# Two-layer hybrid decoder on one core: side work of the attention heads moved to other ticks, q and k of layer 1 transposed as soon as they are scaled

## The chip, the cores and the metric

One core of a Trainium2 chip runs the whole program as one launch. The metric is the device time of that launch in microseconds. Engines: TensorE (PE; its weight loads are shown as PEld), VectorE (DVE), ScalarE (ACT), GpSimd (POOL) and SyncE (SP), which issues most DMAs. Each engine works off its own list of instructions in order.

## The reference

256 positions, model width 2048, two layers, a final RMSNorm, all in fp32. Cut to what matters:

```python
def layer_even(x, norm_g, w_in, w_out):            # layer 0
    h = rmsnorm(x, norm_g)
    qa, ka, va, iq, ik, iw, qb, kb, vb, gate = split_cols(h @ w_in, SPLIT0)
    o_a = dsa_attention(...)      # 10 heads; an indexer picks 64 keys per query
    o_b = dilated_attention(...)  # 6 heads; softmax over strided windows
    return x + (concat(o_a, o_b) * silu(gate)) @ w_out

def layer_odd(x, norm_g, w_in, b_f, w_out):        # layer 1
    h = rmsnorm(x, norm_g)
    qc, kc, vc, qd, kd, vd, fl, gate = split_cols(h @ w_in, SPLIT1)
    o_c = stick_breaking_attention(qc, kc, vc)     # 8 heads
    log_f = log_sigmoid(fl + b_f)
    o_d = forgetting_attention(qd, kd, vd, log_f)  # 8 heads
    return x + (concat(o_c, o_d) * silu(gate)) @ w_out

# stick breaking, per query and head, over the keys before it:
#   z = q.k / sqrt(128); tail = sum of log_sigmoid(-z) over later keys
#   w = exp(log_sigmoid(z) + tail);  o = w @ v
# forgetting: softmax(q.k / sqrt(128) + c[query] - c[key]) @ v, c = cumsum(log_f)
```

## The kernel before

**Jobs.** The projections are cut into jobs, each for the columns of one head (q, k, v, gate: 512 columns) or of some other group: in layer 0 `B0 K I0 I1 B1 B2 B3 A0 A2 A4 A6 A8 B4 B5` (an A job holds q and gate of two heads; K and I belong to the indexer), then `P0` to `P3`, the four column blocks of the output projection; in layer 1 `C0 F1 G1 C2 ... C7 D0 ... D7`, then `Q0` to `Q3`. F1 and G1 are the two halves of head C1; F1 also carries the forget gates. `project` runs one job: 16 steps over the contraction (kt), each with six matmuls of up to 512 columns. fp32 accuracy comes from splitting weights and activations each into a high part and a remainder: `hi x xh`, `hi x xl`, `lo x xh` (lines 324, 325, 327) for two blocks of 128 positions.

**Weights.** SP loads them in pieces of four kt (`raw`, three buffers). `split` turns a half piece (two kt) into `whi` on ACT (line 283) and `wlo` on DVE (line 284), four buffers each, three halves ahead of PE. A piece's buffer is loaded again by a DMA that is put in line four ticks after its second half was split (`later`).

**Ticks.** After each kt of a 512-column job PE's instruction stream has a tick. Between ticks a head's side work is put in line, by generators: `start` runs one up to its first `yield n`, and `advance` resumes it n ticks later. So all engines' lists hold the side work at places counted in ticks; nothing at run time moves an instruction past another one on its engine. After odd kts (two kt are one half) the next `split` follows: an even tick stands in front of a split, an odd one in the middle of a half.

**A head** (`head_b`, `heads_a`, `head_c`, `head_cf`, `head_d`) begins when its job's projection is done (its tick 0) by emptying the two PSUM accumulators: q and k scaled into `qk` (`scaled_qk`, layer 1) or rotated (`rotate`, layer 0), v and the gate (`vg1`: exp on ACT, reciprocal on DVE, `u`). Then q and k are transposed by way of DRAM: DVE transposes 32x32 blocks into `far` (`far`, line 418), SP stores `far` to DRAM (`fard`, line 420) and loads it back in the turned order into `qk` (line 422); `qk_parts` splits it into high part and remainder (`qkh`, `qkf` on ACT, `qkl` on DVE). The gate `u` goes the same way (`gate_turned`). The last head of each layer (B5, D7) has its q, k and gate transposed on PE instead (`turn`).

**Softmax heads** (A, B, D): scores on PE into PSUM tile `s`; `soft` adds the bias, takes the row extreme (`sn`, `nm` on DVE) and the exponential (ACT); `share` scales with the reciprocal row sum (`sc`, DVE); `turn` transposes `sn` on PE into `tp`; `cut` makes `ph` (ACT) and `pl` (DVE), and ACT copies `p1`; `weigh_out` multiplies with v into PSUM tile `o`, DVE multiplies by the gate (`uT`), and `cut` writes `yh` (ACT) and `yl` (DVE), the output projection's input. **Stick heads** (C, `stick_head`): scores into `s`; `z` on DVE, three functions on ACT, `sp` on DVE, `sph` (ACT) and `spl` (DVE); a second group on PE for the running sums; `z` again, exponential, `ph` (ACT), `pl` (DVE); `weigh_out`. The tiles `s`, `o`, `qkf`, `qkh`, `qkl`, `ph`, `pl`, `p1` have one buffer each; `tp` has two. ACT and DVE take turns where both read one accumulator or one turned tile.

`forget` makes the forget gates' running sum on PE; `forget_bias` prepares a D head's bias.

Of the kernel before, what the change touches and what calls it, by code (L numbers as in the profile page):

```python
# [14 lines left out]
P = 128  # L15
# [16 lines left out]
YPOS = {}  # L32
# [141 lines left out]
def trunk(ctx, tc, x, xT, g1, w0, wo0, w1, wo1, bf, gf, consts, rope, out):  # L174
# [232 lines left out]

    def far(srcs, dst, first, done, stored):

        yield first  # L410
        t = hp.tile([P, 512], F32, name="far", tag="rt2")
        ns = [x.shape[1] // P for x in srcs]
        n = sum(ns)
        d = dr.tile([P, P * n], F32, name="fard", tag=f"fard{n}", bufs=4)
        o = t[:, 0:P * n].rearrange("p (j b c) -> p b j c", j=4, b=n)
        for i, x in enumerate(srcs):
            b = sum(ns[:i])
            nc.vector.transpose(o[:, b:b + ns[i]], x.rearrange("p (b j l) -> p b j l", j=4, l=32))  # L418
        yield done
        nc.sync.dma_start(d, t[:, 0:P * n])  # L420
        yield stored
        nc.sync.dma_start(dst.rearrange("p (i f) -> p i f", i=4),
                          d.rearrange("r (j f) -> (r j) f", j=4).rearrange("(i q) f -> q i f", i=4))

    def qk_turned(qk, last, more=0):

        if last:
            yield last
            r = qk_parts(quarters(turn([qk[:, i * P:(i + 1) * P] for i in range(4)])))
            yield 6 - last  # L430
        else:
            yield from far([qk], qk, 1, 3, 4)
            yield 7
            r = qk_parts(arrived(qk, 4))
            yield 3 + more
        return qk_of(r)
# [87 lines left out]

    def softmax_head(qk, nb, v, u, rs, kt, last):
        uT = None if last else gate_turned(u)
        qk = yield from qk_turned(qk, last)
        pr, l = soft(qk, nb() if callable(nb) else nb)
        yield 2
        share(pr, factor(l, rs))  # L530
        yield 2 if last else 4
        pt = turn([pr[:, 0:P], pr[:, P:SEQ], pr[:, SEQ:384]])
        ph = hp.tile([P, SEQ], F32R, name="ph", tag="ph", bufs=1)
        pl = hp.tile([P, SEQ], F32R, name="pl", tag="pl", bufs=1)
        p1 = hp.tile([P, P], F32, name="p1", tag="p1", bufs=1)
        cut((ph, pl), pt[:, 0:SEQ])
        nc.scalar.activation(p1, pt[:, SEQ:384], AF.Copy)
        if last:
            uT = gate_turned_here(u)
        yield 2 if last else 3  # L540
        weigh_out(ph, pl, p1, v, uT, kt, False)
# [57 lines left out]
    def head_b(ps, h):  # L599
# [15 lines left out]
        last = 4 * (h == HB - 1)  # L615
        yield from softmax_head(qk, bmask, v, u, hr0, YPOS[f"B{h}"], last)

# [89 lines left out]
    def heads_a(ps, h):  # L707
# [11 lines left out]
        uT = gate_turned(u.rearrange("p a b c -> p (a b c)"), 4)  # L719
        yield from far([qk], qk, 1, 3, 4)  # L720
        yield 7
        q = arrived(qk, 4)
# [5 lines left out]
        nc.vector.tensor_tensor(quarters(lo), q[:, 2:4], quarters(hi).bitcast(F32), op=OP.subtract)  # L728
        yield 3
        js = [slice(j * P, (j + 1) * P) for j in range(2)]  # L730
# [108 lines left out]
    def forget(ps):  # L839
# [11 lines left out]
        nc.vector.scalar_tensor_tensor(flat(logf), flat(z), 0.0, flat(e), op0=OP.min, op1=OP.subtract)  # L851
        yield 5
        pc = pa.tile([P, 512], F32, name="s", tag="s", bufs=1)
# [23 lines left out]
    def stick_head(qk, v, uT, kt):  # L877
# [23 lines left out]
        pl = hp.tile([P, SEQ], F32R, name="pl", tag="pl", bufs=1)  # L901
        nc.scalar.activation(ph, z[:, P:384], AF.Copy)
        yield 1
        nc.vector.tensor_tensor(pl, z[:, P:384], ph.bitcast(F32), op=OP.subtract)
        yield 3
        weigh_out(ph, pl, z[:, 0:P], v, uT, kt, True)

    def stick(qk, v, u, kt):
        uT = gate_turned(u)
        t = yield from qk_turned(qk, False, 2)  # L910
        yield from stick_head(t, v, uT, kt)

    def head_c(ps, h):
        qk = scaled_qk(ps, 0, (2, 1), (3, 0))
        v, u = yield from vg1(ps, 256, h == 0)
        yield from stick(qk, v, u, h)

    def head_cf(ps, qk):
        v, u = yield from vg1(ps, 0)
        yield from stick(qk, v, u, 1)  # L920

    def head_d(ps, h):
        qk = scaled_qk(ps, 1, (0, 3), (1, 2))
        v, u = yield from vg1(ps, 256)
        last = 3 * (h == HDD - 1)
        yield from softmax_head(qk, lambda: biases[h], v, u, None, HC + h, last)

# [51 lines left out]
    for ji, (_, _, name, _) in enumerate(jobs):  # L979
# [26 lines left out]
        elif k == "I":  # L1006
            start(both(index(ps, h), best()) if h else index(ps, h))
        elif k == "A":
            start(heads_a(ps, h))
        elif k == "P":  # L1010
            start(feed1(ps, h))
        elif k == "F":
            held = scaled_qk(ps, 0, (2, 1), (3, 0))
            start(forget(ps))
        elif k == "G":
            start(head_cf(ps, held))
        elif k == "C":
            start(head_c(ps, h))
        elif k == "D":
            start(head_d(ps, h))  # L1020
        elif k == "Q" and h < 3:
            residual(ps, 2, h)
            start(gain(h))
# [35 lines left out]
```

## Time and profile before

| | |
|---|---|
| median of 3 runs | 917.76 us (917.73 to 918.2) |
| profiled execution | 918.31 us, of which the span shown is 916.5 us |
| PE busy | 897.2 us, 98% |
| DVE, ACT, POOL busy | 644.5, 476.4, 48.7 us |
| granted TensorE clock, mean | 0.994 |
| DMA | 194.20 MB, mean 212 GB/s |

Times in the profile count from the span's start. Matmuls are pipelined and their ends are modelled, so the distance between starts tells more of them than their durations. A row's idle time in brackets is that of the engine just before it, with what ended it. A granted clock of 1.00 is 2.4 GHz, half of it 1.2 GHz.

### The profile page before, as it was taken

Reading aid. Unit: us, or ns where it says so; the run is one execution under the profiler, and the core shown is the slowest. Engines: PE = TensorE matmul, PEld = TensorE weight load, DVE = VectorE, ACT = ScalarE, POOL = GpSimd, SP = SyncE. Lnnn points to the kernel's source line nnn. Section 1 sums busy time; section 2 is a strip of 40 time slices with the busy share of each in tenths; the row PEclk is TensorE's granted clock in tenths of the full one; section 3 lists DMA queues with packets and bytes.
Section 4 is the critical chain, followed back from the end, with each engine's and each line's share of the span. In section 5 each row is a group of like instructions: output and inputs, shape, how many; then the busy total and the mean of one; then the engine's idle time right before and its main releaser. Section 6 shows DMA issues by size and latency. Waiting matters only on the chain.

```text
span 916.5 us, 11926 instructions
## 1 busy us (share of the span) xinstructions
PE 897.2 (98%) x4295; PEld 749.7 (82%) x4295; DVE 644.5 (70%) x1136; ACT 476.4 (52%) x834; POOL 48.7 (5%) x71
## 2 busy tenths in 40 slices
PE   9999999999999998999999999999999999998996
PEld 6988888888888887888898788888778888887886
DVE  7667888777777775666667777767777777775563
ACT  7655544555555554554455555554555555554450
POOL 0021100000000000000000000000000000001110
PEclk9999999999999999999999999999999999999998
DMA  9974455675656653666586666665666666664542
GB/s 356 350 263 148 174 219 186 210 248 207 218 197 216 212 201 138 230 230 230 164 287 230 217 193 202 215 203 190 209 208 229 240 220 219 217 201 138 184 184 92
DMA packets 67355, 194.20 MB, mean 212 GB/s; under 512 B 15952, under 2 KB 38624, under 8 KB 49376
## 3 DMA queue, kind: packets, MB, share of 16 engines
q1 hardware_dynamic: 65856, 190.14, 59.2%
q0 software_dynamic: 864, 2.12, 0.9%
q10 hardware_dynamic: 576, 1.19, 0.4%
q8 instruction: 33, 0.54, 0.2%
q14 instruction: 26, 0.21, 0.1%
HBM read 178.61 MB, written 14.82 MB: 211 GB/s over the span
## 4 chain that ended last, share of the span: by engine, by line
PE 77%; DVE 10%; ACT 5%; issue 4%; DMA 3%; POOL 0%; SPq 0%; DVEq 0%; POOLq 0%; ACTq 0%
PE pj L324 24%; PE pj L325 24%; PE pj L327 24%; DVE wlo L284 4%; ACT whi L283 3%; DVE e L829 2%; PE tp L388 1%; DMA uT<-fard 1%; DMA fard<-far 1%; DMA raw<-in_w_in_dram 1%; DVE far L418 1%; PE o L440 1%; DMA w0yh<-in_w_in_dram 1%; PE s L501 1%; PE s L440 0%
## 5 line engine op out<-in xcount | busy, mean ns | idle before, releaser
L284 DVE TENSOR_TENSOR wlo<-raw,whi 128x1024 fp32r<-128x1024 f32 (+3 forms) x300 | 354.8, 1195 | 177.9 <-ACT whi L283 172.8
L324 PE MATMUL pj<-whi,xh 128*128 128x512 f32 (+3 forms) x992 | 381.1, 386 | 0.2 <-ACT whi L283 0.2
L325 PE MATMUL pj<-whi,xl 128*128 128x512 f32 (+3 forms) x992 | 376.7, 381 | 0.0
L283 ACT ACTIVATE whi<-raw 128x1024 fp32r<-128x1024 f32 (+3 forms) x300 | 298.9, 1022 | 84.7 <-PE pj L325 63.1
L327 PE MATMUL pj<-wlo,xh 128*128 128x512 f32 (+3 forms) x992 | 296.9, 381 | 0.0
L324 PEld LDWEIGHTS pj<-whi,xh 128*128 128x128 f32 x992 | 186.8, 188 | 33.3 <-ACT whi L283 1.4
L327 PEld LDWEIGHTS pj<-wlo,xh 128*128 128x128 f32 x992 | 183.9, 188 | 36.0
L325 PEld LDWEIGHTS pj<-whi,xl 128*128 128x128 f32 x992 | 186.9, 188 | 32.0
L324 PE MATMUL pj<-whi,yh 128*128 128x512 f32 (+1 forms) x248 | 97.0, 391 | 0.0
L325 PE MATMUL pj<-whi,yl 128*128 128x512 f32 (+1 forms) x248 | 96.3, 388 | 0.0
L327 PE MATMUL pj<-wlo,yh 128*128 128x512 f32 (+1 forms) x248 | 77.8, 387 | 0.0
L327 PEld LDWEIGHTS pj<-wlo,yh 128*128 128x128 f32 x248 | 47.5, 191 | 9.4
L325 PEld LDWEIGHTS pj<-whi,yl 128*128 128x128 f32 x248 | 47.4, 191 | 9.0
L324 PEld LDWEIGHTS pj<-whi,yh 128*128 128x128 f32 x248 | 47.4, 191 | 8.9
L509 ACT ACTIVATE sn<-sn,nm 128x128 f32<-128x128 f32 (+1 forms) x48 | 21.5, 449 | 62.8 <-DVE nm L507 62.8
L452 ACT ACTIVATE yh<-uT 128x256 fp32r<-128x256 f32 (+1 forms) x27 | 12.3, 457 | 54.3 <-DVE uT L494 25.2
L545 ACT ACTIVATE sq<-xs 128x512 f32<-128x512 f32 x23 | 14.3, 623 | 29.0 <-DVE xs L768 27.1
L829 DVE RECIPROCAL e<-e 128x256 f32<-128x256 f32 x16 | 28.1, 1753 | 0.5
L383 POOL TENSOR_TENSOR qk<-rot,rot 128x256 f32<-128x256 f32 x16 | 11.6, 739 | 228.5 <-DVE rot L378 181.8
L453 DVE TENSOR_TENSOR yl<-uT,yh 128x256 fp32r<-128x256 f32 (+1 forms) x27 | 12.8, 475 | 14.3 <-ACT yh L452 14.3
L886 ACT ACTIVATE sp<-z 128x384 f32<-128x384 f32 x8 | 4.2, 526 | 34.2 <-DVE z L884 34.2
L866 POOL DMA_DIRECT2D cb<-cTd x8 | 5.8, 720 | 266.5 <-DVE nb L871 261.4
(229 smaller groups left out, 738.0 us busy)
## 6 DMA issues: line engine op xcount, KB each, us to landing
raw<-in_w_in_dram SPq DMA_DIRECT2D x108, 1024.0 KB, 5.1
raw<-in_w_out_dram SPq DMA_DIRECT2D x32, 1024.0 KB, 4.9
fard<-far SPq DMA_DIRECT2D x38, 256.0 KB, 2.1
qk<-fard SPq DMA_DIRECT2D x25, 256.0 KB, 3.8
raw<-in_w_in_dram SPq DMA_DIRECT2D x4, 672.0 KB, 8.8
fard<-far SPq DMA_DIRECT2D x21, 128.0 KB, 3.2
uT<-fard SPq DMA_DIRECT2D x20, 128.0 KB, 5.0
raw<-in_w_in_dram SPq DMA_DIRECT2D x4, 528.0 KB, 3.9
```

Of the source, the lines that this page charges most:

```text
L283: nc.scalar.activation(hi, rw, AF.Copy)
L284: nc.vector.tensor_tensor(lo, rw, hi.bitcast(F32), op=OP.subtract)
L324: nc.tensor.matmul(o, a, wh, start=(kt == 0), stop=False)
L325: nc.tensor.matmul(o, b, wh, start=False, stop=False)
L327: nc.tensor.matmul(o, a, wl, start=False, stop=(kt == KT - 1))
L383: nc.gpsimd.tensor_tensor(dst, t1[:, 0:n], t2[:, 0:n], op=OP.add)
L388: nc.tensor.transpose(pt[:, i * P:(i + 1) * P], s, ident)
L452: nc.scalar.activation(dst[0], src, AF.Copy)
L453: nc.vector.tensor_tensor(dst[1], src, dst[0].bitcast(F32), op=OP.subtract)
L509: nc.scalar.activation(sn[:, s], sn[:, s], AF.Exp, scale=-1.0, bias=nm[:, th:th + 1], accum_out=l[:, th:th + 1])
L545: nc.scalar.activation(j, xs[:, th, c * 512:(c + 1) * 512], AF.Square, accum_out=ss[:, i, th, c:c + 1])
L829: nc.vector.reciprocal(e, e)
```

## The change

Counted in ticks from the end of the head's own projection (a regular job has 16, so a tick 18 is tick 2 of the next job):

| | before | after |
|---|---|---|
| C heads: `far` transpose of q, k; store; reload | 1; 4; 8 | 0; 2; 6 |
| parts; scores; `sp`, `sph`, `spl` | 15; 20; 22 | 10; 14; 16 |
| running sums, `z`, `ph`; `pl`; product with v | 26; 27; 30 | 20; 20; 24 |
| D0 to D6: transpose; store; reload; parts | 1; 4; 8; 15 | 0; 2; 6; 10 |
| scores; scaling; transposes; product | 18; 20; 24; 27 | 14; 16; 20; 23 |
| D7: q, k transposed on PE | 3 | 2 |
| D7: scores; scaling; transposes; product | 6; 8; 10; 12 | 6; 8; 10; 12 |
| B0 to B4: transpose; store; reload; parts | 1; 4; 8; 15 | 2; 4; 8; 12 |
| scores; scaling; transposes; product | 18; 20; 24; 27 | 16; 18; 22; 25 |
| A heads: transpose; store; reload; parts | 1; 4; 8; 15 | 2; 4; 8; 12 |
| scores of both heads; transposes of both; product | 18, 20; 23, 26; 29 | 16, 18; 21, 24; 27 |
| forget gates' running sum; its transpose (from F1's end) | 7; 10 | 15; 18 |

B5 keeps its ticks (transposed at 4, scores 6, scaling 8, transposes 10, product 12). No instruction is added or removed. `far` is split into `grid` (the DVE transpose) and `moved` (store and reload), so that layer 1 can do the first right after `scaled_qk`.

```diff
...
         return t.rearrange("p (i b c) -> p b i c", i=4, b=n)
-    def far(srcs, dst, first, done, stored):
-        yield first
+    def grid(srcs):
         t = hp.tile([P, 512], F32, name="far", tag="rt2")
         ns = [x.shape[1] // P for x in srcs]
         n = sum(ns)
-        d = dr.tile([P, P * n], F32, name="fard", tag=f"fard{n}", bufs=4)
         o = t[:, 0:P * n].rearrange("p (j b c) -> p b j c", j=4, b=n)
         for i, x in enumerate(srcs):
             b = sum(ns[:i])
             nc.vector.transpose(o[:, b:b + ns[i]], x.rearrange("p (b j l) -> p b j l", j=4, l=32))
+        return t[:, 0:P * n]
+    def moved(t, dst, done, stored):
+        n = t.shape[1] // P
+        d = dr.tile([P, P * n], F32, name="fard", tag=f"fard{n}", bufs=4)
         yield done
-        nc.sync.dma_start(d, t[:, 0:P * n])
+        nc.sync.dma_start(d, t)
         yield stored
         nc.sync.dma_start(dst.rearrange("p (i f) -> p i f", i=4),
                           d.rearrange("r (j f) -> (r j) f", j=4).rearrange("(i q) f -> q i f", i=4))
-    def qk_turned(qk, last, more=0):
-        if last:
-            yield last
-            r = qk_parts(quarters(turn([qk[:, i * P:(i + 1) * P] for i in range(4)])))
-            yield 6 - last
-        else:
-            yield from far([qk], qk, 1, 3, 4)
-            yield 7
-            r = qk_parts(arrived(qk, 4))
-            yield 3 + more
+    def far(srcs, dst, first, done, stored):
+        yield first
+        yield from moved(grid(srcs), dst, done, stored)
+    def qk_turned(qk, ticks, last):
+        yield last or ticks
+        r = qk_parts(quarters(turn([qk[:, i * P:(i + 1) * P] for i in range(4)])) if last else arrived(qk, 4))
+        yield 6 - last if last else 4
         return qk_of(r)
     def three_of(o, ah, al, bh, bl, first, last):
...
         for th, s in BLK:
             nc.vector.tensor_scalar(pr[:, s], pr[:, s], sc[:, th:th + 1], None, op0=OP.mult)
-    def softmax_head(qk, nb, v, u, rs, kt, last):
+    def softmax_head(qk, ticks, nb, v, u, rs, kt, last):
         uT = None if last else gate_turned(u)
-        qk = yield from qk_turned(qk, last)
+        qk = yield from qk_turned(qk, ticks, last)
         pr, l = soft(qk, nb() if callable(nb) else nb)
         yield 2
         share(pr, factor(l, rs))
...
             nc.vector.scalar_tensor_tensor(u[:, t], tg[:, t], 1.0, ps[th][:, 384:512], op0=OP.add, op1=OP.mult)
         lower()
         last = 4 * (h == HB - 1)
-        yield from softmax_head(qk, bmask, v, u, hr0, YPOS[f"B{h}"], last)
+        if not last:
+            start(far([qk], qk, 2, 2, 4))
+        yield from softmax_head(qk, 12, bmask, v, u, hr0, YPOS[f"B{h}"], last)
     def keys_a(ps):
         kr = hp.tile([P, 512], F32, name="kr", tag="qk")
...
                                            ps[th][:, 256:512].rearrange("p (a b) -> p a b", a=2),
                                            op0=OP.add, op1=OP.mult)
         uT = gate_turned(u.rearrange("p a b c -> p (a b c)"), 4)
-        yield from far([qk], qk, 1, 3, 4)
-        yield 7
+        yield from far([qk], qk, 2, 2, 4)
+        yield 4
         q = arrived(qk, 4)
         f = hp.tile([P, 256], F32, name="qqf", tag="qkf", bufs=1)
         hi = hp.tile([P, 256], F32R, name="qqh", tag="qkh", bufs=1)
...
         nc.scalar.activation(quarters(hi), q[:, 2:4], AF.Copy)
         nc.scalar.activation(quarters(f), q[:, 0:2], AF.Copy)
         nc.vector.tensor_tensor(quarters(lo), q[:, 2:4], quarters(hi).bitcast(F32), op=OP.subtract)
-        yield 3
+        yield 4
         js = [slice(j * P, (j + 1) * P) for j in range(2)]
         ph, pl = (hp.tile([P, 2, SEQ], F32R, name="pA" + n, tag="i" + n, bufs=1) for n in "hl")
...
         nc.scalar.activation(e, e, AF.Ln, bias=1.0)
         yield 1
         nc.vector.scalar_tensor_tensor(flat(logf), flat(z), 0.0, flat(e), op0=OP.min, op1=OP.subtract)
-        yield 5
+        yield 13
         pc = pa.tile([P, 512], F32, name="s", tag="s", bufs=1)
         nc.tensor.matmul(pc[:, 0:2 * HDD], tri, flat(logf), start=True, stop=False)
         nc.tensor.matmul(pc[:, HDD:2 * HDD], ones, logf[:, 0], start=False, stop=True)
...
         nc.scalar.activation(z, z, AF.Exp)
         ph = hp.tile([P, SEQ], F32R, name="ph", tag="ph", bufs=1)
         pl = hp.tile([P, SEQ], F32R, name="pl", tag="pl", bufs=1)
-        nc.scalar.activation(ph, z[:, P:384], AF.Copy)
-        yield 1
-        nc.vector.tensor_tensor(pl, z[:, P:384], ph.bitcast(F32), op=OP.subtract)
-        yield 3
+        cut((ph, pl), z[:, P:384])
+        yield 4
         weigh_out(ph, pl, z[:, 0:P], v, uT, kt, True)
-    def stick(qk, v, u, kt):
+    def stick(qk, ticks, v, u, kt):
         uT = gate_turned(u)
-        t = yield from qk_turned(qk, False, 2)
+        t = yield from qk_turned(qk, ticks, 0)
         yield from stick_head(t, v, uT, kt)
     def head_c(ps, h):
         qk = scaled_qk(ps, 0, (2, 1), (3, 0))
+        start(moved(grid([qk]), qk, 2, 4))
         v, u = yield from vg1(ps, 256, h == 0)
-        yield from stick(qk, v, u, h)
+        yield from stick(qk, 10 if h else 8, v, u, h)
     def head_cf(ps, qk):
         v, u = yield from vg1(ps, 0)
-        yield from stick(qk, v, u, 1)
+        yield from stick(qk, 10, v, u, 1)
     def head_d(ps, h):
         qk = scaled_qk(ps, 1, (0, 3), (1, 2))
+        last = 2 * (h == HDD - 1)
+        if not last:
+            start(moved(grid([qk]), qk, 2, 4))
         v, u = yield from vg1(ps, 256)
-        last = 3 * (h == HDD - 1)
-        yield from softmax_head(qk, lambda: biases[h], v, u, None, HC + h, last)
+        yield from softmax_head(qk, 10, lambda: biases[h], v, u, None, HC + h, last)
     def tail(ps, c2):
...
             start(feed1(ps, h))
         elif k == "F":
             held = scaled_qk(ps, 0, (2, 1), (3, 0))
+            start(moved(grid([held]), held, 2, 4))
             start(forget(ps))
         elif k == "G":
             start(head_cf(ps, held))
```

What this does to DVE's list in the steady run of C heads (the place is the start of a C head's side work; `spl`, `z`, `pl` belong to the head before it, `qk` to `v` empty the new head's accumulators, `wlo` are weight remainders). Before, the earlier head's chain from `spl` to its product's `uT` and `yl`:

```order
L453 TENSOR_TENSOR spl<-sp,sph 128x384
L284 TENSOR_TENSOR wlo<-raw,whi 128x1024 x2
L898 TENSOR_TENSOR z<-s,z 128x384
L284 TENSOR_TENSOR wlo<-raw,whi 128x1024
L904 TENSOR_TENSOR pl<-z,ph 128x256
L284 TENSOR_TENSOR wlo<-raw,whi 128x1024
L492 TENSOR_TENSOR uT<-o,uT 128x4x32 x2
L453 TENSOR_TENSOR yl<-uT,yh 128x256
```

In the change, from `spl` to `pl`:

```order
L456 TENSOR_TENSOR spl<-sp,sph 128x384
L819 TENSOR_SCALAR qk<-pj_5210,rstd 128x128
L819 TENSOR_SCALAR qk<-pj_5211,rstd 128x128
L416 STREAM_TRANSPOSE far<-qk 128x4x4x32
L833 TENSOR_SCALAR e<-e 128x256
L834 RECIPROCAL e<-e 128x256
L839 SCALAR_TENSOR_TENSOR u<-pj_5210,rstd,e 128x128
L839 SCALAR_TENSOR_TENSOR u<-pj_5211,rstd,e 128x128
L468 SCALAR_TENSOR_TENSOR v<-pj_5210,rstd,v 128x128
L284 TENSOR_TENSOR wlo<-raw,whi 128x1024 x2
L903 TENSOR_TENSOR z<-s,z 128x384
L456 TENSOR_TENSOR pl<-z,ph 128x256
```

`pl` now follows `z` directly, without a `wlo` between; the new head's emptying, with the transpose of its q and k, stands between `spl` and the second `z`.

DVE's list in Q0, where D6 and D7 end. Before, from D6's `pl` (first row) over the scaling of D7 (`sc`, `sn`) to D7's own `pl` and D6's `uT` and `yl`:

```order
L453 TENSOR_TENSOR pl<-tp,ph 128x256
L515 RECIPROCAL sc<-l 128x2
L523 TENSOR_SCALAR sn<-sn,sc 128x128
L523 TENSOR_SCALAR sn<-sn,sc 128x256
L284 TENSOR_TENSOR wlo<-raw,whi 128x1024
L453 TENSOR_TENSOR pl<-tp,ph 128x256
L284 TENSOR_TENSOR wlo<-raw,whi 128x1024
L494 TENSOR_TENSOR uT<-o,uT 128x2x4x32
L453 TENSOR_TENSOR yl<-uT,yh 128x256
```

In the change, from the `wlo` in front of D6's `uT` to D7's `pl`:

```order
L284 TENSOR_TENSOR wlo<-raw,whi 128x1024
L497 TENSOR_TENSOR uT<-o,uT 128x2x4x32
L456 TENSOR_TENSOR yl<-uT,yh 128x256
L518 RECIPROCAL sc<-l 128x2
L526 TENSOR_SCALAR sn<-sn,sc 128x128
L526 TENSOR_SCALAR sn<-sn,sc 128x256
L284 TENSOR_TENSOR wlo<-raw,whi 128x1024
L456 TENSOR_TENSOR pl<-tp,ph 128x256
```

D6's `uT` and `yl` stood behind D7's `pl`; now they stand ahead of D7's scaling.

## Rows read from the trace of the kernel before

**Rows 1.** The page, part 1: busy time of PE, its share of the span, number of instructions.

```profile
PE 897.2 (98%) x4295; PEld 749.7 (82%) x4295; DVE 644.5 (70%) x1136; ACT 476.4 (52%) x834; POOL 48.7 (5%) x71
```

**Rows 2.** The waits of PE over the whole span: what waited, for whom, us in total, times, longest.

```profile
PE o L439 <- DVE uT L494: 5.3, 2, 2.6
PE o L440 <- DVE pl L904: 4.9, 7, 1.2
...
PE s L894 <- ACT sph L452: 0.4, 1, 0.4
...
PE s L895 <- DVE spl L453: 0.2, 1, 0.2
```

**Rows 3.** The view of line 440 (second matmul of a group of three), its part on what the engine waited for: us and times.

```profile
  DVE qkl L398: 0.5, 2
```

**Rows 4.** The timeline of PE during the projection of D1: start us, duration us, engine, line, operation; the first matmul of two neighbouring ticks.

```profile
656.60 0.39 PE L324 MATMUL pj<-whi,xh 128*128 128x512 f32 x1
...
657.96 0.39 PE L324 MATMUL pj<-whi,xh 128*128 128x512 f32 x1
```

**Rows 5.** The timeline of PE in Q0, round the products of D6 (first row) and D7 (fourth row); in brackets idle time before and its releaser.

```profile
830.89 0.28 PE L439 MATMUL o<-ph,v 128*128 128x256 f32 x1
...
831.38 0.48 PE L324 MATMUL pj<-whi,yh 128*128 128x512 f32 x1
...
832.39 0.63 PE L327 MATMUL pj<-wlo,yh 128*128 128x512 f32 x2
835.67 0.36 PE L439 MATMUL o<-ph,v 128*128 128x256 f32 x1 [2.65 <-DVE uT L494]
...
836.24 0.61 PE L324 MATMUL pj<-whi,yh 128*128 128x512 f32 x1
...
840.19 0.63 PE L327 MATMUL pj<-wlo,yh 128*128 128x512 f32 x2
```

**Rows 6.** Windows (us from the span's start): window, its length, busy us (and instructions) of PE, PEld, DVE, ACT, POOL, then the granted clock of PE as a share of the full one, the DMA share and GB/s.

```profile
357.00:362.00 5.00, 4.75 (x16) 3.91 (x17) 2.61 (x5) 1.96 (x4) 0.00 (x0) 0.66 0.00 0
...
640.00:680.00 40.00, 37.66 (x176) 30.98 (x175) 29.20 (x47) 20.93 (x38) 1.63 (x3) 1.00 0.62 199
...
836.00:841.00 5.00, 5.00 (x19) 4.01 (x18) 2.50 (x4) 1.97 (x3) 0.00 (x0) 0.66 0.13 16
```

**Rows 7.** The timelines of ACT (first row) and DVE in Q0: the copy ph of D7, the multiplication uT that follows D6's product, and the yl after it.

```profile
831.50 0.38 ACT L452 ACTIVATE ph<-tp 128x256 fp32r<-128x256 f32 x1 [1.97 <-PE o L441]
...
835.11 0.41 DVE L494 TENSOR_TENSOR uT<-o,uT 128x256 f32<-128x256 f32 x1
836.00 0.42 DVE L453 TENSOR_TENSOR yl<-uT,yh 128x256 fp32r<-128x256 f32 x1 [0.48 <-ACT yh L452]
```

**Rows 8.** The timeline of PE at the product of C4 and the first regular matmul behind it.

```profile
594.17 0.28 PE L439 MATMUL o<-ph,v 128*128 128x256 f32 x1
594.98 0.39 PE L440 MATMUL o<-pl,v 128*128 128x256 f32 x1 [0.52 <-DVE pl L904]
...
595.46 0.48 PE L324 MATMUL pj<-whi,xh 128*128 128x512 f32 x1
```

**Rows 9.** The timelines of DVE and ACT during the projection of C7, work of head C5: the first z and the spl of the softplus, then the second z and ph.

```profile
606.55 0.55 DVE L884 TENSOR_TENSOR z<-s,cons 128x384 f32<-128x384 f32 x1
...
612.04 0.56 DVE L453 TENSOR_TENSOR spl<-sp,sph 128x384 fp32r<-128x384 f32 x1 [0.59 <-ACT sph L452]
...
615.27 0.55 DVE L898 TENSOR_TENSOR z<-s,z 128x384 f32<-128x384 f32 x1
...
616.41 0.42 ACT L902 ACTIVATE ph<-z 128x256 fp32r<-128x256 f32 x1
```

**Rows 10.** The timeline of DVE after the end of C7's projection: the emptying of its accumulators, the next weight remainder, the transpose of q and k.

```profile
623.95 0.60 DVE L814 TENSOR_SCALAR qk<-pj,rstd 128x128 f32<-128x128 f32 x2
625.24 0.29 DVE L828 TENSOR_SCALAR e<-e 128x256 f32<-128x256 f32 x1 [0.69 <-ACT e L824]
...
628.14 1.22 DVE L284 TENSOR_TENSOR wlo<-raw,whi 128x1024 fp32r<-128x1024 f32 x1
629.27 0.70 DVE L418 STREAM_TRANSPOSE far<-qk 128x512 f32<-128x512 f32 x1
```

**Rows 11.** The timeline of DVE in Q0 (D6's and D7's softmax work between weight remainders): first score row, next weight remainder, qkl, reciprocal, weight remainder; then pl of D6 and the weight remainder after it.

```profile
818.73 0.28 DVE L507 CUSTOM_DVE_ANT_0 sn<-s,nb 128x128 f32<-128x128 f32 x1
...
821.02 1.23 DVE L284 TENSOR_TENSOR wlo<-raw,whi 128x1024 fp32r<-128x1024 f32 x1 [1.66 <-ACT whi L283]
822.17 0.55 DVE L398 TENSOR_TENSOR qkl<-tp,qkh 128x384 fp32r<-128x384 f32 x1
822.63 0.15 DVE L515 RECIPROCAL sc<-l 128x2 f32<-128x2 f32 x1
...
823.29 1.22 DVE L284 TENSOR_TENSOR wlo<-raw,whi 128x1024 fp32r<-128x1024 f32 x1
...
827.86 0.42 DVE L453 TENSOR_TENSOR pl<-tp,ph 128x256 fp32r<-128x256 f32 x1
...
829.57 1.23 DVE L284 TENSOR_TENSOR wlo<-raw,whi 128x1024 fp32r<-128x1024 f32 x1 [0.63 <-ACT whi L283]
```

**Rows 12.** Time from issue to landing of DMAs: of q and k's reloads between 595 and 650 us (first row), of all transfers through the turning buffer in DRAM (second row).

```profile
DMA to landing us min/median/max: 4.5/4.9/5.2
DMA to landing us min/median/max: 1.7/3.2/6.8
```

## The prediction

> **What bounds the kernel now.** I read the page's busy times first: TensorE (PE) is busy for 897.2 of 916.5 us [rows 1], so a change that neither adds nor removes a matmul can only gain where PE stands still or runs slowly. Next PE's own waits [rows 2, 3]: a dozen microseconds in few places. Nothing there is a wait for weights worth speaking of; ACT and DVE keep up with the split of the weights, and what PE waits for is side work that was put in line too late.
>
> The regular pace: the same matmul of two neighbouring ticks starts 1.36 us apart [rows 4], so a matmul of 512 columns takes 0.227 us. Everything beyond that is a side group or a loss.
>
> The dearest place is the seam where a layer's last two heads meet its output projection. In Q0 the attention product of D6 starts at 830.89 and that of D7 one tick later [rows 5]. D7's should start 0.45 after 832.39, at 832.84; it starts at 835.67, so 2.83 late, and its group takes 0.57 instead of 0.49. Then the clock falls: ten matmuls from 836.24 to 840.19 take 3.95, where 2.27 and 0.09 for the longer first one are normal, so 1.59 more. The granted clock was 0.66 in that stretch [rows 6]. Together 4.5 us. The cause stands one engine further back [rows 7]: ACT's copy ph of D7 (tick 10) waits 1.97 us until D6's product (tick 11, put in line after it) has read the only ph buffer. The weight copy behind it, DVE's wlo, and D6's uT (835.11), which frees the only o buffer, are late in turn. P0 has the same picture for B4 and B5: the 5.3 us of [rows 2] are two waits, and 357 to 362 shows the same 0.66.
>
> The second place is layer 1's stick-breaking heads: seven of eight wait for pl [rows 2]. A product group of C4 takes 1.29 us from 594.17 to 595.46 [rows 8], against 0.49 without the wait [rows 5]; 0.80 is lost where the view shows 0.52 idle, so 0.28 is hidden in modelled ends. pl stood a tick behind ph, after a weight split.
>
> **The change, part by part.** I count in ticks after the end of a head's own projection, at time T0.
>
> *Seams.* D6's product moves from tick 11 to 7 of Q0, B4's from 11 to 9 of P0, both now ahead of the last head's ph at tick 10. The ph wait, the late uT and the clock's fall go: 2 x 4.5 = 9.0. What is late next? In Q0 the product of D6 (7) now also stands ahead of D7's scaling of its weights (8). DVE must therefore do D6's uT and yl first, and yl waits for ACT. I follow DVE by the steps of [rows 11], from the scores of D6 two ticks before T0 (they end 2.81 before it, DVE follows 0.2 later, an estimate from the 0.15 between uT's end at 835.52 and PE's start at 835.67): sn at -2.6; to wlo 2.29; to the next operation 1.15; sc and scaling 0.66; so D7's qk at 1.5. From there to wlo 4.19 [rows 10] = 5.7; qkl 6.8; wlo 7.3; pl of D6 8.4; to the next wlo 1.71 = 10.1; D7's sn 11.3; wlo 2.29 later, 13.6; uT 14.7; yl 0.89 later, 15.6 [rows 7]; sc 0.33 and scaling 0.74 later, 16.7. PE reaches D7's transposes (tick 10) at 10 x 1.36 plus four side groups at about 0.5: 15.6. So a new wait of 1.1, between 0 (if DVE is that much quicker) and 2.1. In P0 the order is kinder: B5's scaling (8) stands ahead of B4's product (9), and I charge nothing. Seams: 9.0 - 1.1 = 7.9.
>
> *Products of the C heads.* Now lost: 4.9 idle plus 7 x 0.28 hidden = 6.9. The change puts pl straight behind ph at tick 20 and the product at 24, but it also moves the chain towards T0, where a new head empties its projection. Again by steps: scores end at -2.8; z at -2.6; z to spl 5.49 [rows 9], spl at 2.9; next operation 0.5 later, 3.4; from qk to the first wlo 4.19 [rows 10], 7.6; two wlo at 1.13 each; z at 9.8; ph 1.14 later [rows 9]; ph 0.42, pl 0.42; pl ends at 11.8. PE reaches the product after eight ticks, 10.9, one group of four matmuls (1280 columns, 0.57) and 0.09: 11.55, and its second matmul 0.12 later. So a rest of about 0.2 per head. With the chain 0.3 shorter it is nothing, with it 0.6 longer it is the 0.8 of now. I take 0.2: 6.9 - 7 x 0.2 = 5.5 gained; bounds 0 and 6.9.
>
> *Small waits.* 0.4 and 0.2 for sph and spl of one head, 0.5 in two waits for qkl [rows 2, 3]: sph has 4 ticks as before, but starts behind an emptied queue; qkl gets 4 ticks instead of 3. Idle 1.1 plus 4 x 0.28: 2.2 gained, at least 0.
>
> *What I cost at nothing.* The transpose of q and k (0.70) now lies inside the emptying, between qk and e, where DVE idled 0.69 for ACT [rows 10]: covered; without the cover 0.7 would go onto the chain above for each C head. DVE delivers the fourth half's wlo at 7.6 + 1.2 = 8.8; PE wants it three halves (8.16), one group (0.66) and four matmuls (0.91) after T0, at 9.7: 0.9 to spare. The store and reload of q and k are on SP's queue; between them now stands a weight load that waits for that wlo (8.8), so the reload is issued at about 9.3 and lands up to 5.2 later [rows 12], at 14.5; ACT comes to it, behind yh and a weight copy, at about 16.4, and PE needs it at 20.4. The weight load itself goes out 1 us later than now, with three pieces in flight. For the A and B heads the scores fall on the tick of a new head's emptying; their transposed weights keep the same 3 ticks until the product, and one wlo fewer stands ahead of them: nothing, up to 0.3 per head if I am wrong. The running sum of the forget gates moves to a tick at which the scores' buffer is free.
>
> *Sum.* 7.9 + 5.5 + 2.2 = 15.6 against the profiled 918.31: 902.7. The median of the runs is 0.55 below the profiled one: 902.1, forecast 902.
>
> **The clock.** Waits of up to 1.2 us between 640 and 680 left the granted clock at 1.00, the level of 2.4 GHz; the two of 2.65 us brought it to the lower one [rows 2, 6]. My new wait of 1.1 is on the harmless side, so the sum has no term for it. The Trainium skill, page "TensorE: Matmul & The Clock Gate", section "A second HAM failure mode: psum-queue depth-cycling", says that frequent short pauses between groups of matmuls are enough to make the clock swing. By that rule the seven C waits should have cost clock already; the trace disagrees so far. At the new wait it would give the second rival below.
>
> **Rivals.**
> 1. *The C chain is longer than I count* and pl is late again by 0.8: the 5.5 are not gained, 907.5. For it: the slack I found is -0.2, and three of its steps are put together from different heads. Against: pl no longer stands behind a wlo and its whi. Chance 0.17.
> 2. *The clock falls at the new wait in Q0*: 1.6 more, as in [rows 5], 903.6. For it: nothing between 1.2 and 2.65 us was seen. Chance 0.08.
> 3. *The wait in Q0 only changes its cause*: D7's scaling is so late that PE idles 2.7 and the clock falls. Then Q0 loses the 4.5 it loses now instead of 1.1: 905.4. Chance 0.07.
> 4. *The seams don't move*, because something other than ph holds them: 9.0 - 1.1 not gained, 910. Against: the row names PE's product as what ACT waited for [rows 7]. Chance 0.05.
> 5. *Slower*: the reload of q and k, 4 ticks ahead of its use instead of 7, lands late. ACT then stands with the weight copies behind it, and PE's scores wait. Issued at 9.3 and needed, with 1.5 for the copies, at 19, it may take 9.7; every microsecond beyond costs about 1 in each of the 25 heads that reload, so that 15.6 are eaten up at 10.3. Against: the longest of all these transfers took 6.8 [rows 12]. 918 to 930. Chance 0.03.
>
> **How the numbers follow.** The forecast has 0.60, its own range 899.5 (all 18.1 gained) to 904.5 (the C rest at 0.5). Up to rival 1 with a little beyond it, 899 to 909 leaves out rivals 4 and 5 and some edges. This kernel can be told from no change at 0.2%, 1.8 us: faster 0.95, same 0.02 (an edge of rivals 4 and 5), slower 0.03.
>
> **What would show it.** PE's waits: no row for o <- uT; granted clock 1.00 through both seams; one new wait of about a microsecond on the transposes of D7's sn; the row for pl gone or near 1 us in total; ACT's ph in Q0 without idle before it. Wrong would be: pl's row at 4 us or more, a stretch below clock 1.00 after 357 or 820, PE waiting for wlo or whi at the start of layer 1's jobs, or ACT's qkh waiting for a DMA.

## The result and the profile after

The changed kernel takes 905.99 us (905.67 to 906.77) against 917.96 for the kernel before in the same comparison: ratio 0.9871, 95% interval 0.9854 to 0.9888. Forecast were 902 and a range of 899 to 909. The profiled execution took 905.67, of which the span is 903.9; before it was 916.5, so 12.6 are to be found in the profile, where the sum had 15.6.

The page's busy times and PE's waits over the whole span (what waited, for whom, us in total, times, longest), as in [rows 1, 2]:

```profile
PE 892.9 (99%) x4295; PEld 747.0 (83%) x4295; DVE 646.8 (72%) x1136; ACT 475.0 (53%) x834; POOL 50.5 (6%) x71
```

```profile
PE s L976 <- DVE mhalf L972: 1.2, 1, 1.2
PE s L859 <- DVE z L903: 0.9, 1, 0.9
PE tp L388 <- DVE sn L526: 0.8, 1, 0.8
PE pj L324 <- ACT whi L283: 0.4, 1, 0.4
```

The rows for uT and pl are gone. The first and last of these rows belong to the kernel's start. The wait on sn is the one forecast for Q0, the one on z is new and was not forecast.

*Seams.* Q0 round D7's transposes on PE, and ACT's ph there (to set beside [rows 5, 7]):

```profile
819.82 0.61 PE L327 MATMUL pj<-wlo,yh 128*128 128x512 f32 x2
821.28 0.61 PE L388 MATMUL tp<-cons,sn 128*128 128x128 f32 x3 [0.84 <-DVE sn L526]
...
821.86 0.48 PE L324 MATMUL pj<-whi,yh 128*128 128x512 f32 x1
...
821.98 0.38 ACT L455 ACTIVATE ph<-tp 128x256 fp32r<-128x256 f32 x1 [0.76 <-PE tp L388]
```

From the end of the regular pair (819.82 + 0.45) to 821.86 are 1.59 us; the same group in P0 takes 0.47. So 1.12 is lost, where 1.1 was forecast. ACT's ph now waits for its own transposes, not for D6's product. The windows (length; busy us and instructions of PE, PEld, DVE, ACT, POOL; granted clock; DMA share; GB/s) of P0's seam, of the stretch of [rows 6] and of Q0's seam all stand at clock 1.00:

```profile
349.00:355.00 6.00, 6.00 (x33) 5.05 (x32) 3.75 (x6) 2.41 (x6) 0.00 (x0) 1.00 0.50 175
640.00:680.00 40.00, 39.92 (x185) 33.01 (x185) 32.49 (x55) 23.19 (x43) 1.99 (x3) 1.00 0.63 222
819.00:826.00 7.00, 6.16 (x33) 4.91 (x32) 4.90 (x10) 3.25 (x6) 0.00 (x0) 1.00 0.51 179
```

*Products of the C heads.* PE at one of them, with the pl it needs (DVE), to set beside [rows 8]:

```profile
579.88 0.38 PE L442 MATMUL o<-ph,v 128*128 128x256 f32 x1
580.34 0.39 PE L443 MATMUL o<-pl,v 128*128 128x256 f32 x1
...
580.82 0.47 PE L324 MATMUL pj<-whi,xh 128*128 128x512 f32 x1
...
579.86 0.43 DVE L456 TENSOR_TENSOR pl<-z,ph 128x256 fp32r<-128x256 f32 x1 [1.04 <-ACT ph L455]
```

The second matmul starts 0.46 after the first, where 0.12 is normal, and 0.05 after pl's end (580.29). The group takes 0.95 instead of 0.49, in seven of eight heads alike. PE's view of waits has no row for it: the wait lies inside the modelled 0.38 of the first matmul. The same view of PE's weight loads (PEld), which stand in front of the matmuls, has it, seven times:

```profile
PEld o L443 <- DVE pl L456: 1.9, 7, 0.3
...
PEld pj L327 <- DVE wlo L284: 0.8, 2, 0.5
```

A missing row among PE's waits is therefore no proof that nothing waits; the distance between starts tells, and the rows of the weight loads say for whom.

*The forget gates' running sum.* PE, then the DVE and ACT work of C0 that holds the scores' buffer:

```profile
479.95 0.39 PE L325 MATMUL pj<-whi,xl 128*128 128x512 f32 x1
480.44 0.73 PE L327 MATMUL pj<-wlo,xh 128*128 128x512 f32 x2
482.04 0.40 PE L859 MATMUL s<-logf,cons 128*128 128x16 f32 x2 [0.87 <-DVE z L903]
...
481.44 0.55 DVE L903 TENSOR_TENSOR z<-s,z 128x384 f32<-128x384 f32 x1
...
466.56 1.06 ACT L283 ACTIVATE whi<-raw 128x1024 fp32r<-128x1024 f32 x1 [1.99 <-DMA raw<-in_w_in_dram]
```

The group takes 1.62 where it took 0.38: 1.24 lost. z reads the one buffer `s` until 482.0, because C0's whole chain is late; it starts behind a weight copy that waited 1.99 for its DMA. Six of the seven profiled executions that keep the C heads' new ticks bear this out: the copy starts 0.33 to 0.77 after the first matmul of C0's scores, and C0's running sums take 0.66 to 1.11, each time 0.33 or 0.34 more than that (in the seventh, at 1.49, PE loses a part before the running sums).

The late chain costs more in two places that no row of PE's waits names. The wlo matmul at 480.44 starts 0.49 after the one before it instead of 0.23 (the second PEld row above is for it and for one place at the program's start), and C0's running sums take 0.76 instead of 0.59.

The balance: 15.6 forecast, less 7 x 0.26 (0.46 instead of 0.2) = 1.8, less 1.24, makes 12.6, the difference of the spans. These are the two large terms; the 0.26 and 0.17 at C0 are made up for by small gains elsewhere. Added up from the distances between starts, the seams brought 7.9 (forecast 7.9), the products of the C heads 3.9 (5.5) and the small waits 2.2 (2.2).

### The profile page after: what moved, and what is told of

It is laid out like the page before. It is cut to its first block, busy times and chain, and to the rows that moved or that the text cites. A ratio compares the mean times of both kernels' runs of the same rounds, so it can differ in the third digit from the quotient of the medians.

```text
span 903.9 us, 11930 instructions
## 1 busy us (share of the span) xinstructions
PE 892.9 (99%) x4295; PEld 747.0 (83%) x4295; DVE 646.8 (72%) x1136; ACT 475.0 (53%) x834; POOL 50.5 (6%) x71
## 4 chain that ended last, share of the span: by engine, by line
PE 82%; DVE 10%; ACT 4%; issue 3%; DMA 1%; POOL 0%; SPq 0%; POOLq 0%; DVEq 0%; ACTq 0%
PE pj L324 26%; PE pj L325 25%; PE pj L327 25%; DVE wlo L284 3%; DVE e L834 2%; ACT whi L283 1%; PE tp L388 1%; PE o L443 1%; PE s L504 1%; DVE far L416 1%; DMA w0yh<-in_w_in_dram 1%; PE o L491 1%; PE s L444 1%; PE s L443 1%; PE s L442 1%
## 5 line engine op out<-in xcount | busy, mean ns | idle before, releaser
L904 ACT ACTIVATE z<-z 128x384 f32<-128x384 f32 x8 | 4.2, 525 | 29.1 <-DVE z L903 29.1
```

## The experiments

The kernel before ran beside each of them, on two chips: 19 times on the one (median 917.23, 914.8 to 919.8), where before_B_ticks, before_pl_behind_ph, after_D7_transposes_tick_9 and after_product_26 ran, and 33 times on the other (median 916.96, 915.2 to 919.7), where the rest ran; its mean granted clock was 0.992 to 0.999. The expectations below that speak of one chip have this wrong. That spread comes back under the clock. Diffs are against the kernel that a label begins with, and cut to the lines that matter.

**The seams, one at a time.** The B heads' part alone, in `head_b` (`softmax_head` and `qk_turned` take the tick of the parts as an argument, as in the change):

```diff
...
+        if not last:
+            start(far([qk], qk, 2, 2, 4))
-        yield from softmax_head(qk, bmask, v, u, hr0, YPOS[f"B{h}"], last)
+        yield from softmax_head(qk, bmask, v, u, hr0, YPOS[f"B{h}"], last, 12)
```

> The kernel before with the B heads' part alone: transpose, store, reload, parts at 2, 4, 8, 12, scores 16, product 25; layer 1 is untouched. Theory (seam P0 is held by the single ph buffer, which B4's product reads late): the wait of 2.6 us and the low granted clock at 357 to 362 are gone, 4.5 us gained, 913.5; seam Q0 keeps its 4.5. Rival (the clock falls at the start of P0 whatever the wait): only 2.9 gained, 915.1. Rival (a new wait of the kind that Q0 has in the changed kernel): about 3.4 gained, 914.6.

913.28 us; profiled span 912.1, 4.4 below that of the kernel before. The row of PE's waits for uT, and the windows of both seams:

```profile
...
PE o L442 <- DVE uT L497: 2.6, 1, 2.6
...
```

```profile
350.00:358.00 8.00, 8.00 (x41) 6.71 (x40) 4.67 (x9) 5.03 (x9) 0.00 (x0) 1.00 0.35 131
827.00:836.00 9.00, 6.35 (x26) 4.86 (x25) 4.49 (x7) 3.93 (x8) 0.00 (x0) 0.82 0.35 118
```

One of the two waits is gone, and P0 is at full clock; Q0 is as it was. The D heads' part alone, in `head_d`:

```diff
...
         qk = scaled_qk(ps, 1, (0, 3), (1, 2))
+        last = 2 * (h == HDD - 1)
+        if not last:
+            start(moved(grid([qk]), qk, 2, 4))
         v, u = yield from vg1(ps, 256)
-        last = 3 * (h == HDD - 1)
-        yield from softmax_head(qk, lambda: biases[h], v, u, None, HC + h, last)
+        yield from softmax_head(qk, lambda: biases[h], v, u, None, HC + h, last, 10)
```

> The kernel before with the D heads' part alone (transpose of q and k straight after the scaling, store 2, reload 6, parts 10, scores 14, scaling 16, transposes 20, product 23; D7's q and k transposed at 2); the B and C heads are untouched. Theory (seam Q0 is held by the single ph buffer; what is late next is D7's scaling behind D6's uT and yl): wait of 2.6 us in Q0 replaced by one of 0.8 to 1.1 on the transposes of D7's sn, clock 1.00 there; against the profiled span 916.5 the wait's 1.8 and the clock's 1.6 are gained, span about 913.1. Rival (the new wait is of the C heads' making, since their side work moved too): no new wait, 912.0. Rival (the clock falls in Q0 behind the new wait too): about 914.7. Runs of the kernel before spread from 913.0 to 918.0 in span on this chip with a granted clock of 0.999 to 0.993, so that only places in the profile tell these apart, not the median alone.

914.1 us; profiled span 912.2. The waits and Q0's window:

```profile
...
PE o L451 <- DVE uT L506: 2.6, 1, 2.6
...
PE tp L388 <- DVE sn L535: 0.8, 1, 0.8
...
```

```profile
828.00:835.00 7.00, 6.17 (x33) 4.90 (x32) 4.38 (x10) 3.85 (x8) 0.00 (x0) 1.00 0.50 180
```

The new wait in Q0 comes with the D heads alone, so it is not of the C heads' making. To show what it hangs on, D6's product was put behind D7's scaling again, in the changed kernel (`more` is 2 for D6, so tick 9 of Q0):

```diff
...
-        yield 2 if last else 3
+        yield 2 if last else 3 + more
...
```

> The changed kernel with one edit: the product of D6 at tick 9 of Q0 instead of 7, so that D7's scaling stands ahead of D6's uT and yl on DVE. Theory (the wait of 0.8 in the view, 1.1 in lost time, is D7's scaling standing behind them): the row for tp <- sn is gone, 1.1 gained, 904.9. Rival (D7's scaling is late for another reason, its scores or the weight splits ahead of it): the row stays, 906. Rival (uT and yl, now behind, hold up D7's pl and its product): a wait at the product of about 0.5 to 1, 905.4 or more.

905.21 us. The row for sn is gone and the group is back at 0.47; D7's product group is clean at 0.49. The span is only 0.5 shorter than the changed kernel's, since this execution lost 0.46 more at the program's start and 0.36 more at C0's running sums. The place is settled, and its price by the group: 1.12.

**The clock.** In the changed kernel D7's transposes were put one tick earlier, which lengthens the wait and nothing else:

```diff
-        yield 2 if last else 4
+        yield 2 - (last == 2) if last else 4
...
-        yield 2 if last else 3
+        yield 2 + (last == 2) if last else 3
```

> The changed kernel with the transposes of D7's weights in Q0 one tick earlier (9 instead of 10, product still at 12), which only makes the wait there longer: D7's sn is ready at the same time, so PE should wait 1.36 longer, about 2.3 in the row instead of 0.84, with 1.4 us more lost. Theory (the clock falls behind a wait somewhere between 1.2 and 2.65 us, as in both seams before): granted clock about 0.66 behind it and 1.6 us more, 906 + 1.4 + 1.6 = 909.0. Rival (what brought the clock down in the seams was not the length of the wait alone): clock 1.00, 907.4.

908.34 us (907.71 to 909.81). PE in the profiled execution, and the window behind:

```profile
822.47 0.61 PE L388 MATMUL tp<-cons,sn 128*128 128x128 f32 x3 [2.19 <-DVE sn L526]
...
823.05 0.63 PE L324 MATMUL pj<-whi,yh 128*128 128x512 f32 x1
823.49 0.63 PE L325 MATMUL pj<-whi,yl 128*128 128x512 f32 x1
```

```profile
822.00:830.00 8.00, 7.53 (x31) 6.21 (x32) 3.62 (x6) 2.41 (x5) 0.00 (x0) 0.79 0.36 133
```

Behind a wait of 2.19 the clock fell to the lower level (0.44 from start to start instead of 0.23) and 1.6 us went with it: the projection's matmuls of the next 9 us add up to 1.84 beyond the regular pace, and to 0.24 behind the changed kernel's own wait. Behind 0.84 it stayed. With the long wait the times spread over 2.1 us, and those of the kernel before, with two such waits, over 5. The changed kernel once more, on the other of the two chips:

> The changed kernel once more, unaltered, on the chip of the experiments, to compare its spread with that of the kernel before there (spans 913.0 to 918.0, granted clock 0.993 to 0.999). Theory (that spread is the clock's fall behind the two waits of 2.6 us, which comes in some executions and not in others): without such a wait the changed kernel keeps within about 1 us, 905.7 to 906.8. Rival (the chip itself scatters): 3 to 5 us between its fastest and slowest execution.

906.17 us, 905.98 to 906.46, where the kernel before had 915.7 to 919.7 beside it. So on that chip the changed kernel scattered little. That it is the missing long waits which do this is not shown: after_C_old_ticks and after_old_ticks_D0_25 (below), which have no such wait either, spread over 2.3 and 1.7 us there. Of the kernel before, executions with a mean clock of 0.999 had spans of 913.7, 914.3 and 914.8, those with 0.992 and 0.993 had 917.9 and 918.0 (between them it is less sharp: 0.997 goes from 913.0, below all of these, to 916.0). That fits a fall that comes in some executions and not in others; it is inferred from mean clocks, since only the profiled execution of each kernel can be looked into.

The Trainium skill, page "TensorE: Matmul & The Clock Gate", section "A second HAM failure mode: psum-queue depth-cycling", tells of another kernel whose clock swings because PE pauses briefly and often between groups of matmuls. Seven waits of 0.46, about 24 us apart, and one of 1.12 in the changed kernel left it at 1.00 in every window read here; the long single waits are what brought it down. Pauses that come more often are in no run here.

**What the C heads gain from.** In the kernel before, pl alone was put behind ph:

```diff
-        nc.scalar.activation(ph, z[:, P:384], AF.Copy)
-        yield 1
-        nc.vector.tensor_tensor(pl, z[:, P:384], ph.bitcast(F32), op=OP.subtract)
-        yield 3
+        cut((ph, pl), z[:, P:384])
+        yield 4
```

> The kernel before with one edit: in the stick-breaking (C) heads pl is made straight behind ph at tick 26; scores, running sums and products keep their old ticks, both seams are as before. Theory (pl is late only because a weight split stands between ph and pl): all seven late products become clean, group 0.49 instead of about 1.3, 6.9 us gained, 917.96 - 6.9 = 911.1, and no row for pl in PE's waits. Rival 1 (the chain from the scores to pl is itself too long, so that pl needs the earlier scores of the change as well): groups stay at 0.9 or more, at most 3 us gained, 915 to 918. Rival 2 (the lost time of the groups is something else than pl, and the view only names it): nothing gained, 918.

914.64 us. It is none of the three: all products are clean (0.49 to 0.50) and no row names pl, but up to C7's product the kernel has gained only 3.8 of the 6.9, and 1.0 of that goes again at D0's transposes (group 1.22 instead of 0.25). PE's running sums in one head, and the waits:

```profile
609.92 0.44 PE L894 MATMUL s<-sph,tris 128*128 128x384 f32 x1
610.52 0.44 PE L895 MATMUL s<-spl,tris 128*128 128x384 f32 x1
...
611.04 0.39 PE L324 MATMUL pj<-whi,xh 128*128 128x512 f32 x1
```

```profile
...
PE s L895 <- DVE spl L453: 0.6, 4, 0.2
...
```

In five heads the running sums now take 1.10 to 1.16 instead of about 0.7, in C7 1.79. Without the pause at the product, PE comes to them sooner, and spl is late: the wait only moved. So one more edit was added, q and k's transpose straight after their scaling (for F1 likewise), with all ticks of the scores as before:

```diff
...
         qk = scaled_qk(ps, 0, (2, 1), (3, 0))
+        start(moved(grid([qk]), qk, 4, 4))
         v, u = yield from vg1(ps, 256, h == 0)
...
```

> The kernel with pl straight behind ph (run before_pl_behind_ph) with one more edit: in the C heads q and k are transposed straight after the scaling (store at 4, reload at 8), so that this transpose (0.71) no longer stands between the weight remainder and the first z; parts 15, scores 20, sp 22, running sums 26, product 30 are as before. Without this edit a C head took 24.1 us from product to product, 0.5 of it a wait for spl at the running sums; the changed kernel takes 24.05, with its product at tick 26 23.6, which is the pace without a wait. Theory (the transposes on DVE's chain from the emptying to spl make the wait, 0.6 to 0.7 of it, not the ticks of the scores): the running sums' group falls from about 1.1 to between 0.6 and 0.8, 23.6 to 23.8 per head. Rival (the scores must be put in line earlier, as the change does): group 1.0 or more, 24.0 to 24.1 per head.

909.81 us. DVE between the emptying and the first z, with pl alone moved (first four rows) and with the transpose moved too:

```profile
601.55 1.22 DVE L284 TENSOR_TENSOR wlo<-raw,whi 128x1024 fp32r<-128x1024 f32 x1
602.68 0.71 DVE L418 STREAM_TRANSPOSE far<-qk 128x512 f32<-128x512 f32 x1
603.31 1.18 DVE L284 TENSOR_TENSOR wlo<-raw,whi 128x1024 fp32r<-128x1024 f32 x1
604.41 0.55 DVE L884 TENSOR_TENSOR z<-s,cons 128x384 f32<-128x384 f32 x1
```

```profile
598.49 2.35 DVE L284 TENSOR_TENSOR wlo<-raw,whi 128x1024 fp32r<-128x1024 f32 x2
600.76 0.55 DVE L896 TENSOR_TENSOR z<-s,cons 128x384 f32<-128x384 f32 x1
```

The way from the first wlo to z is 2.27 instead of 2.86, and with it the running sums are at 0.59 and the products at 0.49 in C0 to C6: 23.6 us per head, the pace without any wait. For these seven the scores did not have to move. C7 keeps 1.04 at its running sums, and D0's transposes keep 1.20 instead of 0.25; with the D heads' ticks of the change, the C heads' still the old ones, these are 0.70 and 0.25 (after_C_old_ticks, below).

**What the earlier scores cost.** In the changed kernel the product went from tick 24 to 26:

```diff
         cut((ph, pl), z[:, P:384])
-        yield 4
+        yield 6
```

> The changed kernel with one edit: the product of the C heads is put in line two ticks later, at tick 26 instead of 24; ph and pl stay at 20. Theory (each of seven products loses 0.46 because pl arrives about that much too late, though the view of waits shows no row for it): groups go from 0.95 to 0.49, 7 x 0.46 = 3.2 gained, 905.99 - 3.2 = 902.8. Rival (the 0.46 is not a wait for pl but belongs to the place, such as ph and pl sharing the tick with a new head's work): groups stay at 0.95, 906. Rival (uT and yh, now later, hold up ACT's parts of the next head): a new wait of about 0.5 at the scores, 905 or more.

902.89 us, as expected: the groups of C1 to C7 are at 0.49, 3.1 gained. PE at the same product as above:

```profile
581.47 0.28 PE L442 MATMUL o<-ph,v 128*128 128x256 f32 x1
581.59 0.28 PE L443 MATMUL o<-pl,v 128*128 128x256 f32 x1
...
581.96 0.48 PE L324 MATMUL pj<-whi,xh 128*128 128x512 f32 x1
```

Then, alone again, the running sum of the forget gates one tick later:

```diff
-        yield 13
+        yield 14
         pc = pa.tile([P, 512], F32, name="s", tag="s", bufs=1)
```

> The changed kernel with one edit: the forget gates' running sum one tick later (yield 14 instead of 13). Theory (it waits for the one buffer of the scores, which head C0 holds until its second z has read it at 482.0): the group at 480 falls from 1.62 to 0.38 or little more, 1.2 gained, 904.8. Rival (the buffer is not free one tick later either, since C0's chain is about 2 us late as a whole): 0.3 gained or nothing, 905.7 to 906.

906.47 us: nothing gained.

```profile
...
PE o L442 <- ACT ph L455: 0.5, 1, 0.5
```

The wait went to C0's product, whose group with the running sum takes 2.03 instead of 0.87: C0's chain is about 1.2 late as a whole. Why its weights came 1.99 late was not tried. The three edits together (product 26, running sum 15, D6 at 9):

> The changed kernel with three edits: C products at tick 26, forget gates' running sum one tick later, D6's product at tick 9. Theory (the three losses are separate): 3.1 as measured for the first, 1.2 and 1.1 for the others, 905.99 - 5.4 = 900.6. Rival (the first edit moves C0's product and with it the place of the running sum, so that one of the others is not gained): 901.7 to 902.

901.07 us, ratio to the kernel before 0.9832 (0.9819 to 0.9846). Here the running sum is clean (0.37): C0's product, which was put in line with it in the run before, now stands two ticks later. It is 4.9 of the 5.4; PE waited 0.7 more for its first weights at the start of the program. The other way to get there is to leave the C heads' scores at their old ticks (with D6's product at 9 and the forget gates' running sum back at 7):

```diff
...
         t = yield from qk_turned(qk, ticks, 0)
+        yield 1
...
-        yield from stick(qk, 10 if h else 8, v, u, h)
+        yield from stick(qk, 15 if h else 13, v, u, h)
...
```

> The changed kernel with D6's product at tick 9 (905.2 measured), and the C heads back at their old ticks (parts 15, scores 20, sp 22, running sums and pl 26, product 30, forget gates' running sum 7), but with q and k transposed straight after the scaling and pl straight behind ph. Theory (in the C heads the gain comes from these two and not from the earlier scores, which only bring pl's rest of 7 x 0.46 and the 1.2 at C0): 905.2 - 3.2 - 1.2 = 900.8, or up to 1.5 more if spl is late by 0.2 in each head. Rival (without the earlier scores spl is late by 0.5 in each head as with pl moved alone): 905 or more.

901.84 us (901.73 to 903.98): all C groups clean from C1 to C6, C0's running sums at 1.10, and a new wait at D0, whose pl stands behind two weight remainders (group 1.57). With D0's product two ticks later as well (`more` is 2 for D0 too):

> The kernel of after_C_old_ticks (901.84) with the product of D0 two ticks later (25 instead of 23), as for D6. There D0's group took 1.57 because pl stood behind two weight remainders. Theory (only that place is short of time): the group falls to 0.5, 1.1 gained, 900.8. Rival (D0 as a whole is late, because C7's side work at its old ticks fills DVE): the loss goes to D0's uT and the next head, 901.5 to 901.9.

900.98 us (900.57 to 902.25), ratio 0.9821 (0.9803 to 0.984); D0's group is at 0.5. This and the kernel with three edits are the fastest found, and not to be told apart; both are about 5 us below the changed kernel.

## Why the prediction was right, and where not

- **Seams**: right in place, cause and price. Each part of the change was made alone, and its wait went with it. That the ph buffer is the cause rests on the row of what ACT waited for [rows 7], since no run moved D6's or B4's product alone from behind the last head's ph to ahead of it. The new wait in Q0 came where the DVE steps put it (1.12 for 1.1) and left the clock alone, so rivals 2, 3 and 4 did not happen.
- **C products, the rest**: forecast 0.2 per head, measured 0.46. The chain was nearly right (pl ends 11.94 after T0, forecast 11.8), so 0.14 of the 0.26 is its length. The other part is what follows a wait, and the sum had no term for it: PE started 0.05 after pl, and the waiting matmul took 0.22 to the next start instead of 0.12. The sum had charged such a hidden 0.28 to the old wait [rows 8], but not to its own rest. That is 7 x 0.26 = 1.8 of the 3.9 between 902.1 and 905.99; the running sum (below) is 1.24, and 0.87 is that the sum took the median 0.55 below the profiled execution, where it lay 0.32 above. Rival 1, pl late by 0.8, came true in part (0.46).
- **C heads, the cause**: the prediction named only pl's place, "a tick behind ph, after a weight split". The runs show that pl's place gives about half and then spl is late, and that the transpose taken out of DVE's chain gives the rest. The transpose was costed at nothing because DVE's idle 0.69 covers it [rows 10]. That holds for its new place, where DVE of the changed kernel needs 1.30 from qk to e, as before:

```profile
571.80 0.60 DVE L819 TENSOR_SCALAR qk<-pj,rstd 128x128 f32<-128x128 f32 x2
572.44 0.71 DVE L416 STREAM_TRANSPOSE far<-qk 128x512 f32<-128x512 f32 x1
573.10 0.29 DVE L833 TENSOR_SCALAR e<-e 128x256 f32<-128x256 f32 x1
```

  What was missed is the 0.6 that it leaves free at its old place.
- **Forget gates' running sum**: "a tick at which the scores' buffer is free" was wrong, 1.24 lost. The step took C0 for a C head like the others; its chain starts behind a late DMA, and the buffer was held until 482.0, 1.1 after PE had come there.
- **Costed at nothing**: for the reload of q and k and for the A and B heads this was right. No row of ACT's waits has `qkh` wait for a DMA, the A heads' scores and products add up to 11.0 before and after, and the B heads' products stand at 0.49; rival 5 did not happen. The weight remainders did cost something in one place, 0.26 at 480.44: the 0.9 to spare was used up there because C0's chain is late. PE waiting for wlo in layer 1 was one of the signs of being wrong.
- **Small waits**: gone, as forecast.
- **Own range**: its upper end is mis-added. A rest of 0.5 instead of 0.2 in seven heads makes 904.2, not 904.5; nothing else hangs on it.

## What to carry over

A pause of the bounding engine hides the lateness of everything that comes behind it: before crediting an edit with a whole wait, work out what is late next once the pause is gone. When work is moved, count what it frees at its old place as well as what it costs at its new one. And read short waits from the distance between starts and from the rows of the weight loads, since PE's own view of waits can leave out half a microsecond, seven times over.

## What the hardware showed that was not expected

The fall of the granted clock behind a long wait seems not to come in every execution: the kernel before spread over 5 us (914.8 to 919.8) beside the experiments, while in the first comparison its four times lay within 0.5 us (917.73 to 918.2); the changed kernel stayed within 0.5 us beside the experiments and 1.1 us in the first comparison. Beside the experiments the kernel without the waits of 2.6 us thus scatters less. But two further kernels without such a wait spread over 2.3 and 1.7 us (901.73 to 903.98, 900.57 to 902.25), so there is scatter of another origin as well, and what share the clock has in it stays open.
